# Groups 5 and 7 of an SSD layer projected ahead of the scans in half products, and three parts of the output projection beside the last three scans

## The chip, the cores and the metric

The kernel runs on one core of a Trainium2 chip. The metric is the device time of one execution, in microseconds (us); the median of several runs stands for a kernel. Engines are named as in the profile: TensorE (PE, with its weight load PEld), VectorE (DVE), ScalarE (ACT), GpSimd (POOL), and SyncE (SP), which here does nothing but issue DMA transfers, in order.

## What is computed

One inference step of a trunk of two layers with a final RMS norm: 1024 prompt tokens and 8 x 8 sample tokens, 1088 in all, of width 1024, in fp32. Layer 0 is a Mamba-2 (SSD) layer, layer 1 a pooling layer. The change concerns layer 0, which in the reference is:

```
zxbcdt = h @ w_in                                   # h: modulated RMS norm of x
conv = conv_b + sum(xp[:, k:k + L] * conv_w[k] for k in range(4))
xbc_act = silu(conv)                                # x (2048), B and C (8 groups x 128 each)
dt = softplus(dt_raw + dt_bias); A = -exp(a_log)
y, new_ssm = ssd_scan(xs, dt, A, Bm, Cm, ssm_prev)  # h_t = exp(dt A) h + dt x B^T, y = h C
y = y + d_skip * xs
gated = (y * silu(z)).reshape(b, L, 8, 256)
gated = gated * rsqrt(mean(gated * gated, axis=-1) + EPS) * norm_g
out = gated @ w_out
x = x + (1 + gate) * out
```

The scan runs in eight groups (4 heads, one B and one C of 128 states each), the prompt in 8 chunks of 128 tokens, the samples in one step from a given state. Each group has its own RMS norm over its 256 channels.

## The kernel before

**Products.** Channels lie on the 128 partitions, tokens along the columns. Every matrix product is three fp32r matmuls on a high and a low half of each operand: hi x hi, hi x lo, lo x hi (`mm3`, `mm1`, lines 178, 179 and 180). A projection tile of 128 outputs is made in three chunks of columns `CH` (364, 364, 360), 8 k-tiles each: 72 matmuls. A second form takes two tiles at once, split into a 2 x 2 block product with seven half products in place of eight (`fast_pair`, `product`, lines 945 to 947): each half product has 4 k-tiles, two column quarters of 272 and three matmuls, so a pair takes 7 x 24 = 168 narrower matmuls in place of 144. It needs sums of the activations (slots `T`, built once) and sums of the weights, split three products ahead on VectorE and GpSimd (line 172).

**Front.** `FRONT` names eight pairs made in half products ahead of the scans: the gates z of groups 2 to 7, and group 0 whole (`b` is the pair B and C, `x` the pair of x tiles). z of groups 0 and 1 are made plain. A gate goes through `z_chunk` (tanh on ScalarE, one product on VectorE, which gives 2 silu) and is stored to DRAM. A B, C or x tile goes through `conv_tile`: one tap on ScalarE, three on VectorE over 1112 columns (line 343), tanh, one product on VectorE (line 347).

**Scans.** `scan_group(g)` is a generator of steps: per chunk transposes of B and x, decays from a broadcast of the log sums (`acb`, its DMA at line 497), states and rows on TensorE; at the end the samples, the gate product, the group's norm (the sum of squares by matmul at line 677, Ln and Exp on ScalarE, whose result `rsd` is stored), and the rows, unscaled, stored to DRAM (`gyd`). `ssd_layer` weaves scan g, for g of 0 to 6, with the twelve units (a unit is one chunk of a tile, 24 matmuls) of the projection of group g + 1. Scan 7 is woven with output part 0, whose 24 units have 12 matmuls each.

**Output projection.** `w_out` has 16 k-tiles, two for each group; `PARTS` cuts them in four parts of four. For each k-tile `op_stage` loads the row and the broadcast of its group's rs, `op_split` multiplies (line 702) and makes the halves `gh` (line 706) and `gl` (line 707), with norm_g as a scale. `op_unit` makes the 12 matmuls of a chunk and adds the product, times the gate, to x (line 726, for sample columns 729 and 731). x stays in eight slots. Parts 1 and 2 (`op_paced`) and 3 (`last_part`, which also sums the squares for the next norm) follow scan 7 in `ssd_out`. The slots (`NSLOT_A` of 30) hold all of these tiles; the halves `hh`, `hl` of h take 16 of them until the last projection is done. Small blocks of the adaLN projection (`ada_do`) stand between units.

**Order.** The scheduler gives each engine its instructions in the order in which the code emits them, moved where priorities allow; SP carries nearly every load and store of this layer in one queue, in order.

Of the kernel before, what the change touches and what calls it, by code (L numbers as in the profile page):

```python
# [14 lines left out]
P = 128  # L15
# [10 lines left out]
XA = 4  # L26
# [3 lines left out]
AE = 1  # L30
# [16 lines left out]
FRONT = (("z", 2), ("z", 3), ("z", 4), ("z", 5), ("b", 0), ("z", 6), ("x", 0), ("z", 7))  # L47
# [46 lines left out]
class Build:  # L94
# [95 lines left out]
    def setup(self):  # L190
# [24 lines left out]
        self.eps = cp.tile([P, 2], F32, tag="eps", name="eps")  # L215
        nc.vector.memset(self.eps[:, 0:1], EPS)
        nc.vector.memset(self.eps[:, 1:2], 4.0 * EPS)
# [3 lines left out]
        self.psh = cp.tile([P, 16], F32, tag="psh", name="psh")  # L221
        nc.vector.tensor_scalar(self.psh, self.vec[:, V_PS:V_PS + 16], 0.5, None, op0=ALU.mult)
# [16 lines left out]
    def ada_block(self, src):  # L239
# [16 lines left out]
        mp = self.cp.tile([P, 256], F32, tag="mp", bufs=2, name=self.name("mp"))  # L256
# [31 lines left out]
    def ms_log(self, ss, rst, a, n, inv, eps, tag="tr", bufs=2, more=None):  # L288
# [6 lines left out]
        self.nc.scalar.activation(rst[:, a:a + n], ps[:, :n], AF.Ln, bias=self.eps[:, eps:eps + 1], scale=inv)  # L295
# [39 lines left out]
    def conv_tile(self, ti, raw, dst, ncv):  # L335

        nc, n = self.nc, 1112
        rv = raw[:, 1027:1115].rearrange("p (b w) -> p b w", w=11)
        w = [self.cwh[:, 4 * ti + k:4 * ti + k + 1] for k in range(4)]
# [4 lines left out]
        nc.gpsimd.tensor_copy(ncv[:, 0:1, :], raw[:, 1024:1027].unsqueeze(1))  # L344
        nc.gpsimd.tensor_copy(ncv[:, 1:9, :], rv[:, :, 8:11])
# [5 lines left out]
    def raw_tile(self):  # L351
        return self.gp.tile([P, 1115], F32, tag="raw", bufs=3, name=self.name("raw"))
# [13 lines left out]

    def proj_end(self, G, ii, raw):
        dst = self.slots.get("xbc")
        self.conv_tile(G["ti"][ii], raw, dst, G["ncv"][:, ii])
        G["out"].append(dst)  # L370
        if ii == 3:
            self.nc.sync.dma_start(self.io["ncT"][G["g"]], G["ncv"])

    def proj_group(self, G):

        nc = self.nc
        for ii in range(4):
            w = self.stream_next()
            raw = self.proj_begin(G, ii)
            ada = self.ada_do(self.ada_plan[G["g"], ii]) if (G["g"], ii) in self.ada_plan else iter(())  # L380
            for c, (a, n) in enumerate(CH):
                ps = self.mm_tile()
                self.mm3(ps, w, self.hn, CH[c])
                pn = min(a + n, NP) - a
                nc.scalar.activation(raw[:, 3 + a:3 + a + pn], ps[:, :pn], AF.Identity)
                if pn < n:
# [1102 lines left out]
    def op_paced(self, l, acts, nxt):  # L1489
# [6 lines left out]
        for _ in nxt:  # L1496
            pass
# [284 lines left out]
```

## Time and profile before

| | |
|---|---|
| runs | 1655.09, 1656.16, 1655.75 us; median 1655.75 |
| the profiled execution | 1654.85 us, span 1653.1 us |
| granted TensorE clock, mean | 0.992 |
| TensorE busy | 1614.4 us, 98% of the span |
| VectorE, ScalarE, GpSimd busy | 1313.0, 831.6, 469.1 us (79%, 50%, 28%) |
| moved by DMA | 251.07 MB, 152 GB/s on average |

The span is the time from the first to the last record of the profile; the 1.75 us that the execution's time has more lie around it. The 40 slices of the page are 41 us each. TensorE's digit is 9 in all of them but the first, the twentieth (from 785 us, where scan 7 begins) and the last. The front lasts to about 270 us, the scans 0 to 7 to about 860, output parts 1 to 3 follow, then the pooling layer.

### The profile page before, as it was taken

To read this page: it belongs to the slowest core of one execution; us is meant where nothing else is said; L and a number is where in the kernel's file an instruction comes from. 1 tells how busy PE (TensorE), PEld (TensorE's weight loads), DVE (VectorE), ACT (ScalarE), POOL (GpSimd) and SP (SyncE) were. 2 spreads that over 40 slices of the span, in tenths; PEclk is the share of its full clock that TensorE was granted. 3 is DMA by queue.
4 is the path that set the end of the run, shared out by engine and by line. 5 is a ranking of instruction groups with operands and counts; after the bars stand their busy time and mean duration, and the time that the engine had idled before them with its cause. 6 is when DMAs were issued, how large, how long until landed. Compare 5 with 4: busy or idle time off the path is not lost.

```text
span 1653.1 us, 30634 instructions
## 1 busy us (share of the span) xinstructions
PE 1614.4 (98%) x11965; PEld 1537.2 (93%) x11965; DVE 1313.0 (79%) x2176; ACT 831.6 (50%) x1618; POOL 469.1 (28%) x503
## 2 busy tenths in 40 slices
PE   8999999999999999999899999999999999999997
PEld 6899999989898989998789999999999999999997
DVE  6897587878787787888787656999999968577886
ACT  6544335777677767777442116633333234233364
POOL 0124441313131222313010012366666640000241
PEclk9999999999999999999899999999999999999999
DMA  8423226454453534354867123033323359655773
GB/s 342 160 79 111 91 68 219 128 166 145 158 171 120 182 105 146 125 158 141 290 227 254 42 80 133 28 114 124 111 87 112 126 184 364 201 148 173 171 171 120
DMA packets 115969, 251.07 MB, mean 152 GB/s; under 512 B 17488, under 2 KB 58608, under 8 KB 115824
## 3 DMA queue, kind: packets, MB, share of 16 engines
q1 hardware_dynamic: 111792, 236.39, 42.1%
q0 software_dynamic: 4032, 12.72, 4.4%
q8 instruction: 94, 1.54, 0.4%
q14 instruction: 51, 0.42, 0.1%
HBM read 188.87 MB, written 57.98 MB: 149 GB/s over the span
## 4 chain that ended last, share of the span: by engine, by line
PE 64%; DVE 11%; POOL 8%; issue 8%; DMA 5%; ACT 3%; SPq 0%; DVEq 0%; ACTq 0%; POOLq 0%
PE mm L178 12%; PE mm L179 12%; PE mm L180 11%; PE st L947 3%; PE st L945 3%; PE st L946 3%; PE op L1162 2%; PE op L1163 2%; PE op L1161 2%; POOL w L172 2%; PE y L578 2%; PE S L557 2%; PE y L582 1%; PE am L252 1%; POOL sw L911 1%
## 5 line engine op out<-in xcount | busy, mean ns | idle before, releaser
L178 PE MATMUL mm<-hh,wh 128*128 128x364 f32 x720 | 243.0, 337 | 0.0
L180 PE MATMUL mm<-hh,wl 128*128 128x364 f32 x720 | 237.6, 330 | 0.0
L179 PE MATMUL mm<-hl,wh 128*128 128x364 f32 x720 | 237.0, 329 | 0.0
L947 PE MATMUL st<-hh,w 128*128 128x272 f32 x704 | 203.2, 289 | 0.8 <-DVE w L172 0.8
L946 PE MATMUL st<-hl,w 128*128 128x272 f32 x704 | 203.1, 289 | 0.0
L945 PE MATMUL st<-hh,w 128*128 128x272 f32 x704 | 202.9, 288 | 0.0
L947 PE MATMUL st<-t,w 128*128 128x272 f32 x528 | 152.4, 289 | 3.7 <-POOL w L172 2.9
L946 PE MATMUL st<-t,w 128*128 128x272 f32 x528 | 152.2, 288 | 0.7 <-DVE t L1352 0.7
L945 PE MATMUL st<-t,w 128*128 128x272 f32 x528 | 151.7, 287 | 0.0
L178 PEld LDWEIGHTS mm<-hh,wh 128*128 128x128 f32 x720 | 135.3, 188 | 11.1 <-issue 8.1
L343 DVE SCALAR_TENSOR_TENSOR raw<-raw,cwh,raw 128x1112 f32<-128x1112 f32 x96 | 134.1, 1397 | 6.9 <-ACT raw L341 6.4
L179 PEld LDWEIGHTS mm<-hl,wh 128*128 128x128 f32 x720 | 135.5, 188 | 2.0 <-issue 1.6
L180 PEld LDWEIGHTS mm<-hh,wl 128*128 128x128 f32 x720 | 135.3, 188 | 1.4 <-issue 1.4
L565 POOL TENSOR_TENSOR hd<-h,cd 128x256 f32<-128x256 f32 x56 | 51.7, 924 | 290.8 <-DVE h L566 149.2
L947 PEld LDWEIGHTS st<-hh,w 128*128 128x128 f32 x704 | 132.4, 188 | 1.0 <-DVE w L172 1.0
L945 PEld LDWEIGHTS st<-hh,w 128*128 128x128 f32 x704 | 132.8, 189 | 0.3 <-issue 0.3
L946 PEld LDWEIGHTS st<-hl,w 128*128 128x128 f32 x704 | 132.5, 188 | 0.0
L178 PE MATMUL mm<-gh,wh 128*128 128x364 f32 (+1 forms) x384 | 128.3, 336 | 4.0 <-ACT gh L706 4.0
L1162 PE MATMUL op<-b,w 128*128 128x272 f32 x448 | 128.9, 288 | 1.0 <-DVE b L1091 1.0
L1161 PE MATMUL op<-b,w 128*128 128x272 f32 x448 | 129.5, 289 | 0.0
L179 PE MATMUL mm<-gl,wh 128*128 128x364 f32 (+1 forms) x384 | 127.5, 332 | 1.7 <-DVE gl L707 1.7
L1163 PE MATMUL op<-b,w 128*128 128x272 f32 x448 | 129.0, 288 | 0.0
(294 smaller groups left out, 4581.6 us busy)
## 6 DMA issues: line engine op xcount, KB each, us to landing
wr<-win SPq DMA_DIRECT2D x48, 512.0 KB, 3.6
acb<-acd SPq DMA_DIRECT2D x64, 256.0 KB, 3.6
wr<-pin SPq DMA_DIRECT2D x32, 512.0 KB, 3.9
wr<-pout SPq DMA_DIRECT2D x28, 512.0 KB, 5.3
wr<-pout POOLq DMA_DIRECT2D x20, 512.0 KB, 5.8
x<-xT SPq DMA_DIRECT2D x16, 544.0 KB, 6.7
zsd<-z SPq DMA_DIRECT2D x16, 544.0 KB, 3.1
z<-zsd SPq DMA_DIRECT2D x16, 544.0 KB, 4.0
```

The costliest lines, as they stand in the source:

```text
L172: eng.tensor_tensor(out=lo, in0=src, in1=hi.bitcast(F32), op=ALU.subtract)
L178: nc.tensor.matmul(ps[:, :n], hi[:, k, :], ah[:, a:a + n], start=first, stop=False)
L179: nc.tensor.matmul(ps[:, :n], hi[:, k, :], al[:, a:a + n], start=False, stop=False)
L180: nc.tensor.matmul(ps[:, :n], lo[:, k, :], ah[:, a:a + n], start=False, stop=last)
L343: nc.vector.scalar_tensor_tensor(out=acc[:, :n], in0=raw[:, k:k + n], scalar=w[k], in1=acc[:, :n], op0=ALU.mult, op1=ALU.add)
L565: nc.gpsimd.tensor_tensor(out=hd, in0=h[-1], in1=cd.unsqueeze(2).to_broadcast([P, 4, 64]), op=ALU.mult)
L945: nc.tensor.matmul(ps[c][:, :QUART], hi[:, k], xh[:, t], start=(k == 0), stop=False)
L946: nc.tensor.matmul(ps[c][:, :QUART], hi[:, k], xl[:, t], start=False, stop=False)
L947: nc.tensor.matmul(ps[c][:, :QUART], lo[:, k], xh[:, t], start=False, stop=(k == 3))
L1161: nc.tensor.matmul(ps[:, :QUART], hi[:, k], xh, start=k == 0, stop=False)
L1162: nc.tensor.matmul(ps[:, :QUART], hi[:, k], xl, start=False, stop=False)
L1163: nc.tensor.matmul(ps[:, :QUART], lo[:, k], xh, start=False, stop=k == 7)
```

## The change

The list `FRONT` gets four more pairs: B, C and x of groups 5 and 7 are now projected in half products too. Their conv results are stored to DRAM (`xbd`) and loaded back at step 8 of the scan before. The groups projected beside scans are those of `BESIDE` (1, 2, 3, 4, 6). A table `FILL` says how many units stand behind each step of each scan. Behind the projections stand parts 0, 1 and 2 of the output projection: 24, 24 and 16 units beside scans 5, 6 and 7, and the rest of part 2 behind scan 7, the last six of its units after the norm of group 7. Only part 3 stands behind it whole.

For that, the product with rs and norm_g moves into the end of each scan (line 720 of the changed kernel), one step later than the norm; the rows are stored scaled, and `op_split` is a copy and a subtraction. The last group's rows stay in their slots (`last_rows`). x no longer has eight slots: each tile is loaded (two tiles ahead, `XA`), added to, and stored to `x1d` by parts 0 and 1, and loaded again by the next. The last tile projected beside scans goes k by k over three PSUM tiles, so that a pair of slots of h comes free at each k, and the rows of part 0 are loaded and split there (`self.prep`).

In tiles made ahead of the scans, and in all gates, silu is one ScalarE instruction; the taps of such a conv tile run over 1024 columns and 64 sample columns. A gate is applied over halves (544 columns) in place of quarters or chunks. With silu in place of twice silu the eps of the group norm is EPS and no longer 4 EPS, and a halved copy of a scale in the pooling layer is gone. There are four `raw` buffers in place of three and one `mp` buffer in place of two; the adaLN blocks stand beside tiles of projections 1 to 4 and 6, and two in part 0. The conv tiles made beside scans keep tanh.

```diff
-XA = 4
+PREP = ((6, 10, 14, 18, 21), (9, 12, 15, 18, 21))
...
-FRONT = (("z", 2), ("z", 3), ("z", 4), ("z", 5), ("b", 0), ("z", 6), ("x", 0), ("z", 7))
+FRONT = (("z", 2), ("z", 3), ("z", 4), ("b", 5), ("x", 5), ("z", 5), ("b", 7), ("x", 7), ("z", 6), ("b", 0), ("x", 0),
+         ("z", 7))
+BESIDE = (1, 2, 3, 4, 6)
+
+FILL = (((1,) * 10 + (2,),) * 4 + ((1,) * 9 + (4, 5),) + ((3, 2, 2, 2, 2, 2, 2, 2, 2, 2, 3),) * 2 + ((2, 2, 2, 1, 1, 1, 1, 1, 2, 2, 1),))
 WIDE = 1223
...
+        if not scan:
+            w = [self.vec[:, V_CW + 4 * ti + k:V_CW + 4 * ti + k + 1] for k in range(4)]
+            sd = dst[:, NP:TOK].rearrange("p (b i) -> p b i", i=8)
+            for k in range(4):
+                for d, r in ((dst[:, :NP], raw[:, k:k + NP]), (sd, rv[:, :, k:k + 8])):
+                    if k:
+                        nc.vector.scalar_tensor_tensor(out=d, in0=r, scalar=w[k], in1=d, op0=ALU.mult, op1=ALU.add)
+                    else:
+                        nc.scalar.activation(d, r, AF.Identity, bias=self.vec[:, V_CB + ti:V_CB + ti + 1], scale=w[0])
+            nc.scalar.activation(dst, dst, AF.Silu)
...
+            if (G["g"], ii) == (BESIDE[-1], 3):
+
+                ps = [self.mm_tile() for _ in CH]
+                for k in range(8):
+                    for c in range(3):
+                        self.mm1(ps[c], w, k, self.hn[k], CH[c], k == 0, k == 7)
+                    self.slots.free(*self.hn[k])
+                    if k:
+                        next(self.prep, None)
+                    if k < 7:
+                        yield
+                for c in range(3):
+                    self.proj_evict(G, ii, raw, ps[c], c)
+                yield
+                return
...
         nc.sync.dma_start(self.rsd[g], rs.rearrange("(j q) n -> j q n", q=32)[:, 0, :])
+        self.slots.free(*sq)
+        rst = self.slots.get("rs")
+        nc.sync.dma_start(rst, self.rsd[g].rearrange("j n -> (j n)").unsqueeze(0).to_broadcast([P, TOK]))
+        yield
+
         for q in range(2):
-            nc.sync.dma_start(self.gyd[2 * g + q], xs[q])
-        self.slots.free(*sq, *xs)
+            nc.vector.scalar_tensor_tensor(out=xs[q], in0=xs[q], scalar=self.vec[:, V_SG + 2 * g + q:V_SG + 2 * g + q + 1], in1=rst,
+                                           op0=ALU.mult, op1=ALU.mult)
+            if g < 7:
+                nc.sync.dma_start(self.gyd[2 * g + q], xs[q])
+        self.slots.free(rst)
+        if g < 7:
+            self.slots.free(*xs)
+        else:
+            self.last_rows = xs
         yield
...
+    def op_stage(self, k):
+
+        if k > 13:
+            return self.last_rows[k - 14]
+        raw = self.slots.get("gr", short=True)
+        self.nc.sync.dma_start(raw, self.gyd[k])
+        return raw
+
+    def op_split(self, raw):
+        hi, lo = self.slots.get("gh", F32R, short=True), self.slots.get("gl", F32R, short=True)
+        self.nc.scalar.activation(hi, raw, AF.Copy)
+        self.nc.vector.tensor_tensor(out=lo, in0=raw, in1=hi.bitcast(F32), op=ALU.subtract)
         self.slots.free(raw)
         return hi, lo
...
+    def op_part_load(self, part, out):
+
+        st = None
+        for k in range(*PARTS[part]):
+            nx = self.op_stage(k)
+            if st is not None:
+                out.append(self.op_split(st))
             st = nx
             yield
+        out.append(self.op_split(st))
+        yield
...
+        return self.nc.scalar.activation(dst[:, a:a + n], src, AF.Silu)
...
+                        if g:
+                            t = G["out"].pop()
+                            nc.sync.dma_start(self.xbd[g][ii + i], t)
+                            sl.free(t)
...
+        T, rest = {0: self.G[0]["out"]}, iter(())
+        self.x = [None] * 8
+        self.acts = [[] for _ in PARTS]
+        self.prep = self.op_part_load(0, self.acts[0])
+        self.fill = self.beside(T)
+        for g in range(8):
+            sc = self.scan_group(g, T[g])
+            for i, n in enumerate(FILL[g]):
+                next(sc)
+                for j in range(n):
+                    next(self.fill)
+                    if i in (0, 3) and j == 0:
+                        next(rest, None)
+                if i == 8 and g + 1 in self.G:
+                    T[g + 1] = [sl.get("xbc") for _ in range(4)]
+                    for t, d in zip(T[g + 1], self.xbd[g + 1]):
+                        nc.sync.dma_start(t, d)
+            rest = sc
+        self.prep = self.op_part_load(3, self.acts[3])
+        self.out_unit()
+        next(rest)
+        for _ in range(2):
+            next(self.fill)
+        self.out_unit()
         for _ in rest:
             pass
...
+    def out_unit(self):
+
+        ins = next(self.fill, None)
+        with self.tc.issue_after(ins.ins) if ins else contextlib.nullcontext():
+            next(self.prep, None)
+        return ins
+
+    def beside(self, T):
+
+
+        for g in BESIDE:
+            G = self.proj_open(g)
+            T[g] = G["out"]
+            yield from self.proj_group(G)
+        for p in range(3):
+            for _ in self.prep:
+                pass
+            self.prep = iter(())
+            if p < 2:
+                self.prep = self.op_part_load(p + 1, self.acts[p + 1])
+            for i, ins in enumerate(self.op_units(p)):
+                if p < 2 and i in PREP[p]:
+                    with self.tc.issue_after(ins.ins) if ins else contextlib.nullcontext():
+                        next(self.prep, None)
+                yield ins
+            self.free_acts(self.acts[p])
 
     def free_acts(self, acts):
         for hi, lo in acts:
...
+    def load_x(self, p, d):
+        if d < 8:
+            self.x[d] = self.slots.get("x")
+            self.nc.sync.dma_start(self.x[d], (self.x1d if p else self.io["xT"])[d])
+
+    def op_units(self, p):
+
+        for d in range(XA):
+            self.load_x(p, d)
         for d in range(8):
-            if ada and d + XA < 8:
-                self.load_x(d + XA)
-            if len(acts) > 4:
-                w = self.stream_next()
-            elif d % 2 == 0:
+            if d > 7:
+                if (p, d) in self.ada_late:
+                    for _ in self.ada_do(self.ada_late[p, d]):
+                        pass
+                    yield None
+                continue
+            self.load_x(p, d + XA)
+            if d % 2 == 0:
                 ws = self.stream_pair()
-            blk = self.ada_do(ada[d - 1]) if 0 < d <= len(ada) else iter(())
+            blk = self.ada_do(self.ada_late[p, d]) if (p, d) in self.ada_late else iter(())
             for i, ch in enumerate(CH):
-                ins = self.op_unit(l, self.x, d, w if len(acts) > 4 else ws[d % 2], acts, ch)
+                ins = self.op_unit(0, self.x, d, ws[d % 2], self.acts[p], ch)
                 if i:
                     next(blk, None)
                 yield ins
+            if p < 2:
+                self.nc.sync.dma_start(self.x1d[d], self.x[d])
+                self.slots.free(self.x[d])
```

The first place is on TensorE, where part 0 begins. Before, that is the start of scan 7, behind the last projection (`mm` of `hh` and `hl`) and one adaLN block (`am`); `tr` are the scan's transposes, `gh` and `gl` the halves of the rows, `wh` and `wl` those of the weights:

```order
L178 MATMUL mm_9116<-hh_734,wh_8782 128x360
L179 MATMUL mm_9116<-hl_735,wh_8782 128x360
L180 MATMUL mm_9116<-hh_734,wl_8783 128x360
L252 MATMUL am_9155<-wr_8786,scp 32x256 x4
L252 MATMUL am_9155<-wr_9001,scp 32x256 x4
L514 MATMUL tr_9214<-xbc_8715,xbc_8510 128x128
L518 MATMUL tr_9214<-kc,xbc_8972 128x128
L178 MATMUL mm_9243<-gh_9171,wh_9005 128x364
L179 MATMUL mm_9243<-gl_9172,wh_9005 128x364
```

In the changed kernel it is the start of scan 5, behind the projection of group 6:

```order
L182 MATMUL mm_8402<-hh_739,wh_8149 128x360
L183 MATMUL mm_8402<-hl_740,wh_8149 128x360
L184 MATMUL mm_8402<-hh_739,wl_8150 128x360
L182 MATMUL mm_8547<-gh_8434,wh_8391 128x364
L183 MATMUL mm_8547<-gl_8435,wh_8391 128x364
L184 MATMUL mm_8547<-gh_8434,wl_8392 128x364
L182 MATMUL mm_8547<-gh_8449,wh_8391 128x364
L183 MATMUL mm_8547<-gl_8450,wh_8391 128x364
L184 MATMUL mm_8547<-gh_8449,wl_8392 128x364
L182 MATMUL mm_8547<-gh_8484,wh_8391 128x364
L545 MATMUL tr_8567<-xbc_8364,xbc_8363 128x128
L549 MATMUL tr_8567<-kc,xbc_8365 128x128
```

Part 0 now follows the last projection directly: seven matmuls of its first unit stand ahead of the scan's first transposes, where before the transposes stood first.

The second place is VectorE at the last rows for part 3. Before, these are multiplied and split during part 2; `x` with `mm` is a unit's addition, `wl` the low half of a weight:

```order
L729 TENSOR_TENSOR gs_10808<-mm_10794,gat_266 128x64
L731 TENSOR_TENSOR x_9199<-x_9199,gs_10808 128x64
L702 TENSOR_TENSOR gr_10759<-gr_10759,rs_10699 128x1088
L136 TENSOR_TENSOR wl_10817<-wr_10712,wh_10816 128x1024
L726 SCALAR_TENSOR_TENSOR x_9200<-mm_10822,gat_266,x_9200 128x364
L707 SCALAR_TENSOR_TENSOR gl_10813<-gr_10759,vec,gh_10812 128x1088
L726 SCALAR_TENSOR_TENSOR x_9200<-mm_10836,gat_266,x_9200 128x364
```

In the changed kernel these rows are group 7's own (`xbc`), scaled at the end of scan 7:

```order
L743 TENSOR_TENSOR gl_11149<-gr_11121,gh_11148 128x1088
L720 SCALAR_TENSOR_TENSOR xbc_10195<-xbc_10195,vec,rs_11068 128x1088
L720 SCALAR_TENSOR_TENSOR xbc_10196<-xbc_10196,vec,rs_11068 128x1088
L764 SCALAR_TENSOR_TENSOR x_10975<-mm_11152,gat_271,x_10975 128x364
L743 TENSOR_TENSOR gl_11167<-xbc_10195,gh_11166 128x1088
L764 SCALAR_TENSOR_TENSOR x_10975<-mm_11170,gat_271,x_10975 128x296
L767 TENSOR_TENSOR gs_11184<-mm_11170,gat_271 128x64
L140 TENSOR_TENSOR wl_11194<-wr_11074,wh_11193 128x1024
L769 TENSOR_TENSOR x_10975<-x_10975,gs_11184 128x64
L743 TENSOR_TENSOR gl_11188<-xbc_10196,gh_11187 128x1088
L764 SCALAR_TENSOR_TENSOR x_10307<-mm_11199,gat_271,x_10307 128x364
```

The two products with rs now stand in front of the additions of part 2's last units (the one from `mm_11152` first), and the two splits, with those additions and a weight's split, behind them.

The third place is SP's queue. Before, in scan 7, beside part 0:

```order
L1487 DMA x_9203<-xT 128x1088
L119 DMA wr_9450<-adaA 128x1024
L497 DMA acb_9481<-acd 128x4x128
L497 DMA acb_9572<-acd 128x4x128
L486 DMA h_157_9767<-h0T 128x1024
L119 DMA wr_9452<-adaA 128x1024
L119 DMA wr_9454<-adaG 128x1024
L486 DMA h_158_9769<-h0T 128x1024
L481 DMA z_9828<-zsd_143 128x1088
```

In the changed kernel, in scan 6, beside part 1:

```order
L1521 DMA x_9667<-x1d_165 128x1088
L528 DMA acb_9703<-acd 128x4x128
L1521 DMA x_9544<-x1d_164 128x1088
L666 DMA hsT<-h_164_9162 128x1024
L713 DMA rsd_126<-z_9208 4x272
L1544 DMA x1d_161<-x_9434 128x1088
L1521 DMA x_9750<-x1d_166 128x1088
L716 DMA rs_9524<-rsd_126 128x1088
L1544 DMA x1d_162<-x_9436 128x1088
L737 DMA gr_9766<-gyd_81 128x1088
L528 DMA acb_9779<-acd 128x4x128
L1521 DMA x_9881<-x1d_167 128x1088
```

Between the loads of `acb` now stand loads and stores of x (lines 1521 and 1544), the store and broadcast of rs (713, 716) and loads of rows (737), where weights of adaLN blocks, states and gates stood.

212 lines of the change are left out of this document (59 added, 153 removed).

## The prediction

> **What bounds the kernel now.** I read the page first, then the busy time by windows, then TensorE's waits in the stretches where its share drops.
>
> ```profile
> span 1653.1 us, 30634 instructions
> PE 1614.4 (98%) x11965; PEld 1537.2 (93%) x11965; DVE 1313.0 (79%) x2176; ACT 831.6 (50%) x1618; POOL 469.1 (28%) x503
> ```
> TensorE (PE) is busy for all but 38.7 us. So the time moves by two things: how long its matmuls take, and how long it stands idle. The windows give both; the columns are the window, its length, busy us and instructions of each engine, granted clock, DMA share and GB/s.
>
> ```profile
> 356.00:430.00 74.00, 73.36 (x567) 66.69 (x566) 58.87 (x91) 53.21 (x118) 18.44 (x27) 1.00 0.49 151
> ...
> 782.00:802.00 20.00, 12.71 (x70) 10.76 (x69) 15.79 (x18) 8.92 (x11) 1.17 (x2) 0.74 0.94 327
> 802.00:882.00 80.00, 78.79 (x631) 67.98 (x630) 63.40 (x124) 34.47 (x76) 10.64 (x10) 1.00 0.72 244
> ...
> 900.00:1000.00 100.00, 100.00 (x605) 100.00 (x604) 58.66 (x106) 22.20 (x25) 11.91 (x15) 1.00 0.21 71
> 1040.00:1050.00 10.00, 7.99 (x38) 7.42 (x38) 8.32 (x29) 8.23 (x25) 4.59 (x13) 0.83 0.00 0
> 1100.00:1200.00 100.00, 100.00 (x801) 99.92 (x800) 94.80 (x144) 30.20 (x60) 65.25 (x51) 1.00 0.34 117
> 178.00:262.00 84.00, 82.62 (x659) 82.40 (x658) 64.05 (x108) 33.49 (x57) 36.20 (x37) 1.00 0.24 83
> ```
> 900:1000 holds plain matmuls alone (128x364 and 128x360): 100 us / 605 = 0.1653 us each. 1100:1200 holds half products alone (128x272): 100 / 801 = 0.1248 us each. 356:430 is one scan with twelve projection units beside it: 73.4 of 74 us busy. 782:802 is the worst stretch inside the kernel, where scan 7 and output part 0 begin: 7.3 us idle, clock 0.74, DMA share 0.94.
>
> ```profile
> PE mm L178 <- ACT gh L706: 4.0, 1, 4.0
> PE tr L518 <- DVE xbc L347: 1.8, 1, 1.8
> PE mm L179 <- DVE gl L707: 1.7, 2, 1.4
> ```
> There (waits between 770 and 882) TensorE waits for the first halves of the scan's rows and for its last conv tile.
>
> **The change: matmuls.** Eight projection tiles leave the plain form: 8 x 72 = 576 matmuls x 0.1653 = 95.2 us. Four pairs come in the half-product form: 4 x 168 = 672 x 0.1248 = 83.9 us. The sum is 11.3 us less. All other matmuls keep their number: the scans now carry 24 + 24 + 24 output units of 12 in place of three projections and part 0.
>
> **Idle that goes.** In 782:802 the rows must pass the norm of the group before (rs), then a product with it, then hi and lo, and slots come free only after the whole last projection. Now the scaling is done inside each scan, part 0 needs only groups 0 and 1, finished long before, and the last projection tile goes k by k, so that slots come free while it runs. The 7.3 us go. The clock of 0.74 over 20 us is 10.4 us at half speed (0.26 x 20 / 0.5); some 3.5 us of those lie in the idle time, so 6.9 us at half speed cost 3.4 us more. Together 10.7 us. What is late next, in the order shown above: the four splits and the last two conv tiles share VectorE.
>
> ```profile
> L343 DVE SCALAR_TENSOR_TENSOR raw<-raw,cwh,raw 128x1112 f32<-128x1112 f32 x96 | 134.1, 1397 | 6.9 <-ACT raw L341 6.4
> L347 DVE SCALAR_TENSOR_TENSOR xbc<-raw,raw 128x1024 f32<-128x1024 f32 x32 | 39.9, 1248 | 13.8 <-ACT raw L346 13.8
> L726 DVE SCALAR_TENSOR_TENSOR x<-mm,gat,x 128x364 f32<-128x364 f32 x64 | 37.9, 593 | 30.1 <-PE mm L180 30.1
> L707 DVE SCALAR_TENSOR_TENSOR gl<-gr,vec,gh 128x1088 fp32r<-128x1088 f32 x16 | 23.2, 1451 | 6.8 <-ACT gh L706 4.9 <-DMA hsT<-h 1.9
> L1044 DVE TENSOR_TENSOR pw<-gin,ph 128x1088 fp32r<-128x1088 f32 x16 | 20.2, 1284 | 0.0
> ```
> Four splits at 1.28 (the kind of L1044), one conv tile at 3 x 1.40 + 1.25 and about 5 us of scan work make 15.6 us; the tile's 72 matmuls and the first units' 24 give 96 x 0.165 = 15.8 us of cover. I take +1.5 us, with ends of 0 and the 7.3 that is there now.
>
> **The tail of scan 7.** Before, parts 1 to 3 stood behind it, and its own rows were wanted only by part 3. Now only six units of part 2 stand between its norm and part 3, which wants them at once.
>
> ```profile
> 779.36 1.28 ACT L300 ACT_TABLE_LOAD   x1 [0.45 <-PE ms L677]
> 780.66 0.49 ACT L680 ACTIVATE z<-ms,eps 128x272 f32<-128x272 f32 x1
> 781.18 0.43 ACT L308 ACTIVATE z<-z 128x272 f32<-128x272 f32 x1
> ```
> ```profile
> spl<-spool SPq DMA_DIRECT2D x16, 60.0 KB, 2.1
> rs<-rsd SPq DMA_DIRECT2D x8, 544.0 KB, 6.1
> ```
> From the norm's matmul: 2.2 us on ScalarE, a small store (spl's 2.1 us is the nearest row), the broadcast at 6.1: 10.4 us. Then VectorE, in the order shown: two products (1.45 each), an eviction (0.59), a split (1.28), about 2.2 us of eviction and weight split, the last split (1.28): 8.3 us, so 18.7. Cover: 6 x 12 + 24 matmuls x 0.165 = 15.9 us. The stall is 2.8 us, with ends of 0 (broadcast in 3.3) and 7 (in 10). The unit queued behind the two products on VectorE waits too: a PSUM tile comes free only with it.
>
> ```profile
> 1042.97 0.44 PE L178 MATMUL pl<-hh,wh 128*128 128x360 f32 x1 [1.99 <-ACT hh L318]
> ```
> A gap of this size has a price beside it: after 1.99 us idle the clock in 1040:1050 is 0.83, which is 3.4 us at half speed, 1.7 us. I add it: 4.5 us for the tail. The Trainium skill, "TensorE: Matmul & The Clock Gate", HAM oscillation, asks only that no gap exceed about 3.4 us; by that rule the stall would cost no clock, and the forecast would be 1.7 us lower. The row above speaks against it. The Trainium skill, "ScalarE: Activation LUTs", What ACT_TABLE_LOAD costs, adds 1.38 us of drain to each load; that would put the tail at 5.9 us. Here the next ScalarE instruction starts 1.30 us after the load, so the trace does not agree.
>
> **The front.** Four of twelve pairs are new. The window 178:262 is b, z, x, z of group 0: VectorE 64.1 of 84 us. A conv tile costs it 3 x 1.40 + 1.25 + 0.2 = 5.65 us now and 3 x 1.46 = 4.4 with silu (three products over 1024 and 64 columns). In that window two conv pairs take 22.6 us of it and two gates 9.2 (16 products at 0.574), which leaves 8.1 us per pair for the rest; so a conv pair will take 16.9 of 21 us and a gate pair 8.1. VectorE stays below TensorE, but a conv comes as a lump of 8.8 us, and weights are split three products (9 us) ahead.
>
> ```profile
> PE st L947 <- POOL w L172: 1.4, 1, 1.4
> PE st L947 <- DVE w L172: 0.8, 1, 0.8
> ```
> These are all the waits for weights in the front (93 to 270). Four more conv pairs stand here; I take one such wait for all of them, 1.5, with ends of 0 and 6 (one for each). The silu edits elsewhere I put at nothing: ScalarE takes 0.65 us for 544 columns where it took 2 x 0.43, VectorE loses a product, and TensorE at 100% in 1100:1200 covers both. Extra table loads in the front (1.28 us each) lie on a ScalarE that is busy 33 of 84 us.
>
> **Scans 5, 6 and 7.** VectorE in a scan: 58.9 now, less four conv tiles (22.6), plus 24 evictions (16 x 0.59 + 8 x 0.96), four splits (5.1), two scalings (2.9): 61.3 of 74 us. Scan 7 carries only 16 units: TensorE 74 - 49 + 32 = 57 us against about 53 on VectorE, with less slack. The queue is the larger risk.
>
> ```profile
> acb<-acd SPq DMA_DIRECT2D x64, 256.0 KB, 3.6
> x<-xT SPq DMA_DIRECT2D x16, 544.0 KB, 6.7
> gr<-gyd SPq DMA_DIRECT2D x16, 544.0 KB, 5.9
> x<-x1d SPq DMA_DIRECT2D x8, 544.0 KB, 7.5
> wr<-wout SPq DMA_DIRECT2D x16, 512.0 KB, 4.9
> ```
> In scan 6 SyncE's queue holds 30 transfers of 544 KB (x in and out, the rows, the spilled tiles), 8.5 of acb and 10 of 512 KB: 24 MB, where 356:430 moved 151 x 74 = 11 MB. At 327 GB/s, reached in 782:802, that takes 73 us of 74. x is asked for two rows of units (six units, 12 us and the scan's work) ahead, acb one chunk ahead. I take +3 us for the three scans, ends 0 and 15.
>
> **The sum.** The profiled execution took 1654.85 us (span 1653.1 and 1.75 around it), 0.9 below the median of 1655.75. 1654.85 - 11.3 - 10.7 + 1.5 + 4.5 + 1.5 + 3 = 1643.4; beside the median 1644. The ends of the unknown terms give 1633 (all at 0) to about 1662 (all at their worst, which will not meet).
>
> **The rivals.**
> *The wait only moves* (0.17): scan 5 begins with part 0, where the same loads, conv tiles and splits meet. 96 x 0.165 of cover against 15.6 us of VectorE is level, and a row that lands 6 us late tips it. Then 7.3 + 3.4 stay in place of 1.5: 1653.
> *All hidden* (0.13): the broadcast lands in 3.3 us, scans and front as covered as 356:430: 1634.
> *The queue bounds scans 5 and 6* (0.12, the slower side): transfers stand in order on one queue, stores waiting for evictions ahead of loads. In 802:882 it moved 244 GB/s at share 0.72 with TensorE hardly idle, so more was not asked for; 327 at 0.94 is a burst of 20 us with waits. If a scan's 24 MB come at 244 GB/s, each takes 98 us, 24 more: 1644 + 48 = 1692. It decides for slower from 6 us per scan, 24 MB in 80 us: 300 GB/s.
> That nothing moved is excluded by the order of instructions: 672 more half-product matmuls stand on TensorE.
>
> **Chances.** The forecast has 0.58. Up to 0.2% (3.3 us, about what this measurement can tell) counts as same. Faster: 0.58 + 0.13 + 0.10 of the first rival = 0.81; same: 0.07 of it and 0.01 of the queue's = 0.08; slower 0.11. The range 1633 to 1655 holds all but the queue's case and a little above: 8 in 10 or somewhat more.
>
> **What would show it.** Right: 1456 matmuls on each line of the half product; about 0.125 us each; no wait over 2 us where part 0 begins; a wait of 2 to 4 us for the last rows of scan 7 and a dip of the clock behind it; DMA share near 0.9 in scans 5 and 6 with TensorE above 97%. Wrong: TensorE below 95% in those scans with waits that go back to x or acb (the queue), or the clock low where part 0 begins (the wait moved), or waits of more than 2 us for weights in the front.

## The result and the profile after

| | before | changed |
|---|---|---|
| median | 1655.95 us (4 runs) | 1633.49 us (4 runs, 1629.32 to 1633.99) |
| ratio, 95% interval | | 0.9861, 0.9845 to 0.9876 |
| once more, beside the experiments | 1655.07 us | 1631.56 us; 0.9853, 0.9836 to 0.9869 |
| profiled execution | 1654.85 us | 1633.98 us |

The change gains 22.5 us of medians, or 20.9 from profile to profile. The forecast was 11.5 from profile to profile. The page of the changed kernel, its span and its engines, and below them two of the groups:

```profile
span 1632.2 us, 30956 instructions
PE 1601.1 (98%) x12061; PEld 1524.7 (93%) x12061; DVE 1290.3 (79%) x2140; ACT 816.7 (50%) x1565; POOL 495.2 (30%) x527
...
L982 PE MATMUL st<-hh,w 128*128 128x272 f32 x832 | 240.8, 289 | 2.3 <-DVE w L176 2.3
L982 PE MATMUL st<-t,w 128*128 128x272 f32 x624 | 179.6, 288 | 0.0
```
The half-product form stands there as forecast: 832 + 624 = 1456 on each of its lines. TensorE is idle for 31.1 us, 7.6 less than before.

Busy time by windows, changed kernel: the front's half products, scans 5, 6 and 7 (norm to norm), and the half products of the pooling layer.

```profile
96.00:354.60 258.60, 256.26 (x2036) 254.22 (x2035) 195.74 (x329) 110.62 (x176) 124.87 (x119) 1.00 0.30 103
...
739.00:812.80 73.80, 73.80 (x568) 66.69 (x566) 64.82 (x122) 42.57 (x96) 12.16 (x11) 1.00 0.87 297
812.80:882.10 69.30, 69.27 (x528) 65.33 (x526) 59.39 (x114) 36.55 (x84) 13.05 (x11) 1.00 0.93 327
882.10:941.80 59.70, 55.19 (x427) 50.06 (x425) 46.54 (x91) 29.76 (x75) 10.26 (x9) 0.97 0.61 209
...
1057.00:1352.00 295.00, 295.00 (x2352) 295.00 (x2351) 249.29 (x369) 96.51 (x166) 175.80 (x136) 1.00 0.40 133
```
Scans 5 and 6 are full for TensorE at a DMA share of 0.87 and 0.93. Scan 7 is not. TensorE's waits from the first scan to the end of the output projection (changed kernel):

```profile
PE S L588 <- ACT Bt L566: 4.5, 3, 2.3
PE mm L182 <- ACT raw L419: 2.1, 1, 2.1
PE y L613 <- DVE h L593: 1.4, 1, 1.4
```
The second is the beginning of part 0, the first is scan 7. No wait is listed for the tail behind scan 7. The one at `y`, in scan 0, has its like before, where the scan waited 1.4 us for `M`.

Where the time went, by stages cut at the same instructions in both traces (the last ends with TensorE's last matmul, 8.6 and 8.4 us before the span's end):

| stage | before | changed | difference | forecast |
|---|---|---|---|---|
| start, to the first half product | 93.6 | 96.2 | +2.7 | 0 |
| front, to the first chunk of scan 0 | 175.3 | 258.7 | +83.4 | +85.4 |
| scans and output projection | 753.0 | 649.1 | -103.9 | -96.9 |
| pooling layer, plain pair | 54.6 | 53.7 | -0.9 | 0 |
| pooling layer, half products | 297.7 | 294.9 | -2.8 | 0 |
| the rest | 270.4 | 271.2 | +0.8 | 0 |

### The profile page after: what moved, and what is told of

It reads as the page before. It is cut to its first block, busy times and chain, and to the rows that moved or that the text cites. A ratio compares the mean times of both kernels' runs of the same rounds, so it can differ in the third digit from the quotient of the medians.

```text
span 1632.2 us, 30956 instructions
## 1 busy us (share of the span) xinstructions
PE 1601.1 (98%) x12061; PEld 1524.7 (93%) x12061; DVE 1290.3 (79%) x2140; ACT 816.7 (50%) x1565; POOL 495.2 (30%) x527
## 4 chain that ended last, share of the span: by engine, by line
PE 82%; DVE 7%; DMA 5%; issue 3%; ACT 2%; POOL 1%; SPq 0%; DVEq 0%; ACTq 0%; POOLq 0%
PE st L982 11%; PE st L980 11%; PE st L981 11%; PE mm L182 10%; PE mm L184 10%; PE mm L183 10%; DMA acb<-acd 2%; PE op L1197 2%; PE op L1198 2%; PE op L1196 2%; PE y L609 2%; PE S L588 2%; PE y L613 2%; PE am L253 1%; PE tr L549 1%
## 5 line engine op out<-in xcount | busy, mean ns | idle before, releaser
L982 PE MATMUL st<-hh,w 128*128 128x272 f32 x832 | 240.8, 289 | 2.3 <-DVE w L176 2.3
L980 PE MATMUL st<-hh,w 128*128 128x272 f32 x832 | 240.2, 289 | 0.0
L981 PE MATMUL st<-hl,w 128*128 128x272 f32 x832 | 239.7, 288 | 0.0
L982 PE MATMUL st<-t,w 128*128 128x272 f32 x624 | 179.6, 288 | 0.0
L980 PE MATMUL st<-t,w 128*128 128x272 f32 x624 | 179.6, 288 | 0.0
L981 PE MATMUL st<-t,w 128*128 128x272 f32 x624 | 179.2, 287 | 0.0
L182 PE MATMUL mm<-hh,wh 128*128 128x364 f32 (+1 forms) x528 | 178.4, 338 | 0.1
L184 PE MATMUL mm<-hh,wl 128*128 128x364 f32 (+1 forms) x528 | 174.6, 331 | 0.0
L183 PE MATMUL mm<-hl,wh 128*128 128x364 f32 (+1 forms) x528 | 173.7, 329 | 0.0
L174 ACT ACTIVATE w<-wr 128x512 fp32r<-128x512 f32 x104 | 65.6, 631 | 190.4 <-PE st L982 156.8
L982 PEld LDWEIGHTS st<-hh,w 128*128 128x128 f32 x832 | 156.4, 188 | 3.4 <-DVE w L176 3.4
L980 PEld LDWEIGHTS st<-hh,w 128*128 128x128 f32 x832 | 156.7, 188 | 0.3 <-issue 0.3
L184 PE MATMUL mm<-gh,wl 128*128 128x364 f32 (+1 forms) x384 | 127.1, 331 | 0.0
L980 PEld LDWEIGHTS st<-t,w 128*128 128x128 f32 x624 | 117.7, 189 | 0.0
L982 PEld LDWEIGHTS st<-t,w 128*128 128x128 f32 x624 | 117.3, 188 | 0.0
```

The lines of the kernel that those rows point to most:

```text
L174: self.nc.scalar.activation(hi, src, AF.Copy)
L182: nc.tensor.matmul(ps[:, :n], hi[:, k, :], ah[:, a:a + n], start=first, stop=False)
L183: nc.tensor.matmul(ps[:, :n], hi[:, k, :], al[:, a:a + n], start=False, stop=False)
L184: nc.tensor.matmul(ps[:, :n], lo[:, k, :], ah[:, a:a + n], start=False, stop=last)
L980: nc.tensor.matmul(ps[c][:, :QUART], hi[:, k], xh[:, t], start=(k == 0), stop=False)
L981: nc.tensor.matmul(ps[c][:, :QUART], hi[:, k], xl[:, t], start=False, stop=False)
```

## The experiments

Each was timed in five rounds beside the kernel before; the ratios are to that (median 1655.3 us beside the first four, 1655.07 beside the last four).

| kernel | median us | ratio | 95% interval |
|---|---|---|---|
| silu_only | 1650.85 | 0.9969 | 0.9959 to 0.998 |
| norm_order | 1652.57 | 0.9982 | 0.9974 to 0.9991 |
| front8 | 1640.82 | 0.9911 | 0.9897 to 0.9924 |
| evict_first | 1629.21 | 0.984 | 0.9826 to 0.9853 |
| tail_short | 1633.45 | 0.9862 | 0.9844 to 0.988 |
| cd_late | 1624.93 | 0.9818 | 0.9802 to 0.9834 |
| after_again | 1631.56 | 0.9853 | 0.9836 to 0.9869 |
| x_twice | 1651.59 | 0.998 | 0.9968 to 0.9992 |

### The silu edits alone (silu_only)

```diff
     def z_chunk(self, dst, src, a, n):
 
-        nc = self.nc
-        t = self.mt.tile([P, 416], F32, tag="mt", bufs=2, name=self.name("zt"))
-        nc.scalar.activation(t[:, :n], src, AF.Tanh, scale=0.5)
-        return nc.vector.scalar_tensor_tensor(out=dst[:, a:a + n], in0=t[:, :n], scalar=1.0, in1=src, op0=ALU.add, op1=ALU.mult)
+        return self.nc.scalar.activation(dst[:, a:a + n], src, AF.Silu)
```
The conv tiles ahead of the scans, eps and the pooling scale change with it, as in the change.

> The kernel before with the silu edits alone: gates and the conv tiles ahead of the scans by one silu on ScalarE, gates over halves, the factors of two and eps to match; FRONT, the scans and the output parts stay as they were. Theory A (VectorE relieved of a product in each gate and each of these conv tiles splits the weights in time): the waits for weights go, 0.8 and 1.4 us in the front and three of 0.7 to 0.9 in the pooling layer, 4.5 us in all: about 1651.5. Rival (the prediction's: silu is worth nothing where TensorE is the bound): 1656 within 1, with these waits in place.

Measured: 1650.85, 4.5 below the 1655.3 beside it. TensorE's waits in the pooling layer's half products, in the kernel before:

```profile
PE st L947 <- POOL w L172: 1.5, 2, 0.9
PE st L947 <- POOL u L784: 0.8, 1, 0.8
```
In silu_only no wait is left in that stretch. The same two stages by windows, the front's and the pooling layer's half products, in the kernel before:

```profile
93.30:268.50 175.20, 172.11 (x1364) 170.23 (x1363) 141.14 (x251) 69.67 (x132) 71.48 (x65) 1.00 0.29 100
1076.00:1374.00 298.00, 295.64 (x2355) 294.78 (x2354) 270.10 (x425) 99.48 (x193) 176.25 (x136) 1.00 0.39 132
```
and in silu_only:

```profile
96.20:267.90 171.70, 171.29 (x1364) 170.12 (x1363) 109.56 (x197) 69.87 (x116) 71.95 (x65) 1.00 0.29 102
1076.80:1371.00 294.20, 294.20 (x2353) 294.20 (x2352) 247.75 (x369) 96.29 (x165) 176.09 (x136) 1.00 0.39 134
```
The third busy column is VectorE: 141.1 becomes 109.6 us in the front and 270.1 becomes 247.8 in the pooling layer. With VectorE at 91% of a stretch (270.1 of 298.0) the products that prepare weights and windows came late now and then, although TensorE was the bound. The waits in the pooling layer name GpSimd, which is busy 176 us there in both kernels; but GpSimd itself waits for VectorE's splits of weights, 87.8 us in that stretch before and 72.0 in silu_only. That VectorE's relief reaches TensorE on this way is argued from these rows; no run isolates it.

Cut at the same instructions, the front and the pooling stretch are 3.5 us shorter each; the start is 2.9 longer (below). Theory A holds; the prediction's zero does not. The waits for weights in the front are one in silu_only and, with twelve pairs there, five short ones in the changed kernel (line by line):

```profile
PE st L955 <- DVE w L172: 0.4, 1, 0.4
PE st L982 <- DVE w L176: 2.3, 5, 0.6
```

### The table loads at a scan's start (norm_order)

```diff
-        with self.ln_set(mm):
-            nc.scalar.activation(rs, ps[:, :272], AF.Ln, bias=self.eps[:, 1:2], scale=1.0 / 256)
-            self.rstd(rs)
+        nc.scalar.activation(rs, ps[:, :272], AF.Ln, bias=self.eps[:, 1:2], scale=1.0 / 256)
+        self.rstd(rs)
```

> The kernel before without the table load issued by hand ahead of each group's norm, so that Ln stands ahead of the tanh of the first conv tile on ScalarE, as in the changed kernel: 22 table loads in place of 33, two in place of four at the start of each scan. Theory B (the loads delay Bt, and TensorE waits 0.64 us for it in scans 1 to 6): those six waits go, 3.9 us: about 1652. Rival (the transposes or VectorE's xd end as late): 1656 within 1.

ScalarE at the start of scan 2 in the kernel before (the timeline: start, length, line, operation, the idle time before it):

```profile
423.27 1.28 ACT L300 ACT_TABLE_LOAD   x1 [1.40 <-PE ms L677]
424.56 1.28 ACT L346 ACT_TABLE_LOAD   x1
425.85 1.13 ACT L346 ACTIVATE raw<-raw 128x1112 f32<-128x1112 f32 x1
427.00 1.28 ACT L680 ACT_TABLE_LOAD   x1
...
429.17 1.28 ACT L308 ACT_TABLE_LOAD   x1
...
430.80 0.26 ACT L535 ACTIVATE Bt<-tr 128x128 f32<-128x128 f32 x1
```
and at the same place in the changed kernel:

```profile
511.33 1.28 ACT L301 ACT_TABLE_LOAD   x1 [1.07 <-PE ms L708]
512.62 0.49 ACT L711 ACTIVATE z<-ms,eps 128x272 f32<-128x272 f32 x1
513.13 1.28 ACT L359 ACT_TABLE_LOAD   x1
514.42 1.13 ACT L359 ACTIVATE raw<-raw 128x1112 f32<-128x1112 f32 x1
515.46 0.41 ACT L309 ACTIVATE z<-z 128x272 f32<-128x272 f32 x1
```
Before, a load put there by hand for Ln and Exp (L300) was followed at once by the conv tile's tanh, which loaded its own table; Ln and Exp then loaded again. Four loads, 5.1 us, stood ahead of `Bt`, and TensorE waited for it 0.64 us in each of six scans. In the changed kernel Ln comes first, and two loads do: after tanh, Exp needs none. The Trainium skill, "ScalarE: Activation LUTs", Table sets: the hidden batching unit, lists exp with tanh in one set and exp with ln in another; by that, Ln, tanh, Exp need two loads, and the trace of the changed kernel agrees; in the kernel before, Exp (L308) loads again even behind Ln's own load (L680), which a set with both would have spared. In norm_order the kernel before has the changed kernel's order, and its waits from scan 0 to the end of scan 6 are

```profile
PE y L578 <- DVE M L529: 0.7, 1, 0.7
PE S L557 <- ACT Bt L535: 0.2, 1, 0.2
```
The six waits are gone. A scan of 74.27 us takes 73.85: 0.42 less, where the wait was 0.64. Six times that is 2.5, and the median is 2.7 us lower (1.5 to 4.3 by the interval) where 3.9 was expected. Theory B holds, with a gain nearer 3.

### Eight pairs in front, all else changed (front8)

```diff
-FRONT = (("z", 2), ("z", 3), ("z", 4), ("b", 5), ("x", 5), ("z", 5), ("b", 7), ("x", 7), ("z", 6), ("b", 0), ("x", 0),
-         ("z", 7))
-BESIDE = (1, 2, 3, 4, 6)
+FRONT = (("z", 2), ("z", 3), ("z", 4), ("z", 5), ("b", 0), ("z", 6), ("x", 0), ("z", 7))
+BESIDE = (1, 2, 3, 4, 5, 6, 7)
...
```
`FILL` and the units behind scan 7 are changed to match.

> The changed kernel with the eight pairs of before ahead of the scans and groups 5 and 7 projected beside scans as plain matmuls (576 of them in place of 672 half-product ones); part 0 then begins in scan 6, part 1 stands behind scan 7. All else as changed. Theory C (the form of the matmuls is worth its 11 to 12 us, and scan 7 with 24 units in place of 16 has no waits of its own, worth up to 6): 1633.5 + 11.9 = 1645, less up to 6: 1639 to 1645. Rival (what was gained is waits, and the half-product form gains little): within 3 of the changed kernel's 1633.5.

Measured: 1640.82, 7.3 to 9.3 above the two medians of the changed kernel. The front is 87.2 us shorter (171.5 for 258.7), the scans and the output projection 93.8 longer. So the four pairs do pay, by some 8 us; and nearly two thirds of the whole gain (14.5 us) is there without them. Scan 7, with 24 units in place of 16, still waits:

```profile
792.70:869.70 77.00, 73.27 (x525) 66.58 (x523) 64.57 (x118) 33.03 (x71) 10.12 (x9) 0.96 0.77 269
```
That is one wait of 3.7 us on `Bt` and a stretch of 6.8 us at half speed behind it. More units alone do not cover scan 7.

### Where part 0 begins (evict_first)

```diff
-                for k in range(8):
+                for k in range(5):
                     for c in range(3):
                         self.mm1(ps[c], w, k, self.hn[k], CH[c], k == 0, k == 7)
...
                 for c in range(3):
+                    for k in range(5, 8):
+                        self.mm1(ps[c], w, k, self.hn[k], CH[c], False, k == 7)
                     self.proj_evict(G, ii, raw, ps[c], c)
...
```

> The changed kernel with the last tile's last three k-tiles done chunk by chunk, so that its first PSUM tile is read out while the other two are still summed. Theory D (the first unit of part 0 waits 2.06 us for a PSUM tile because its reading stands on ScalarE behind the split of the fourth row, and the clock's dip follows the wait): 2 to 3.7 us less than the changed kernel, 1630 to 1631.5, with no wait over 0.5 us there. Rival (the fourth row's transfer is what is late): the wait moves to its high or low half and the time stays at 1633.5.

ScalarE in the changed kernel, where the last projection ends at 729.9 us:

```profile
729.80 1.11 ACT L742 ACTIVATE gh<-gr 128x1088 fp32r<-128x1088 f32 x1 [0.88 <-DMA gr<-gyd]
730.81 0.68 ACT L556 ACTIVATE M<-acb,tka 128x128 f32<-128x128 f32 x2
731.40 0.19 ACT L574 ACTIVATE cd<-acb 128x4 f32<-128x4 f32 x1
731.50 0.45 ACT L419 ACTIVATE raw<-mm 128x364 f32<-128x364 f32 x1
```
The first PSUM tile is read out (L419) only behind the fourth row's high half, which waited for its transfer. In evict_first the reading stands ahead of it:

```profile
728.28 0.45 ACT L424 ACTIVATE raw<-mm 128x364 f32<-128x364 f32 x1
728.64 1.12 ACT L747 ACTIVATE gh<-gr 128x1088 fp32r<-128x1088 f32 x1
```
The wait for the tile is gone. Another of 1.4 us stands there now, for a low half on VectorE (`gl`): the rival's wait, in a smaller size. The time fell by 2.4 to 4.3 us, and the profile has no half-speed stretch there or in scan 7. Not all of that is this edit's place: from profile to profile 6.1 us went, 0.6 of waiting and 1.7 of clock where part 0 begins, and 2.0 and 1.7 in scan 7, which the edit does not touch. Whether scan 7 gained by it or by chance, the run does not tell.

### Scan 7 (cd_late)

```diff
-            nc.scalar.activation(M[:L, :, :L], M[:L, :, :L], AF.Exp, scale=-1.0)
+            mx = nc.scalar.activation(M[:L, :, :L], M[:L, :, :L], AF.Exp, scale=-1.0)
...
-                nc.scalar.activation(cd, acb[:, :, 127], AF.Exp)
+                with self.tc.issue_after(mx.ins) if g == 7 else contextlib.nullcontext():
+                    nc.scalar.activation(cd, acb[:, :, 127], AF.Exp)
```
It is laid on evict_first.

> The kernel of evict_first with one edge more: in scan 7, cd of a chunk stands on ScalarE behind the Exp of that chunk's M, no longer ahead of it. Theory F (in scan 7 cd, which needs the acb of a chunk further on, stands on ScalarE in front of work on the chunk at hand, so that a late acb stops TensorE for 4.5 us in all): these waits fall to under 1.5 us: 1 to 3 us below evict_first. Rival (acb itself is late for M and ea, wherever cd stands): the waits stay and so does the time, within 1 of evict_first.

ScalarE in scan 7 of the changed kernel, ahead of the longest wait:

```profile
899.98 0.68 ACT L556 ACTIVATE M<-acb,tka 128x128 f32<-128x128 f32 x2
902.23 0.21 ACT L574 ACTIVATE cd<-acb 128x4 f32<-128x4 f32 x1 [1.56 <-DMA acb<-acd]
902.34 0.61 ACT L557 ACTIVATE M<-M 128x512 f32<-128x512 f32 x1
902.88 0.28 ACT L566 ACTIVATE Bt<-tr 128x128 f32<-128x128 f32 x1
```
`cd` takes 0.2 us but needs the acb of a later chunk, and M and `Bt` of the chunk at hand stand behind it. Two of the three waits in scan 7, 2.35 and 1.35 us, end so; the third, 0.8, stands behind `ea`, which itself waited for its acb. With `cd` moved back, all waits of cd_late from scan 0 to the end of the output projection are

```profile
PE mm L183 <- DVE gl L749: 0.7, 1, 0.7
PE y L619 <- DVE h L599: 0.6, 1, 0.6
PE y L619 <- DVE h L603: 0.4, 1, 0.4
PE S L594 <- ACT Bt L571: 0.2, 1, 0.2
```
Scan 7 takes 53.6 us, where it takes 55.9 in evict_first, with waits of 1.85 and 0.7, and 59.7 in the changed kernel. So theory F holds, and in these profiles the edit is worth 2.3 us in scan 7; the median, 1624.93, is 4.3 below evict_first, more than the 1 to 3 expected, and the rest of that is not explained. It is below both kernels of this study: ratio 0.9818, 0.9802 to 0.9834.

### Three units less behind scan 7 (tail_short)

```diff
-FILL = (((1,) * 10 + (2,),) * 4 + ((1,) * 9 + (4, 5),) + ((3, 2, 2, 2, 2, 2, 2, 2, 2, 2, 3),) * 2 + ((2, 2, 2, 1, 1, 1, 1, 1, 2, 2, 1),))
+FILL = (((1,) * 10 + (2,),) * 4 + ((1,) * 9 + (4, 5),) + ((3, 2, 2, 2, 2, 2, 2, 2, 2, 2, 3),) * 2 + ((2, 2, 2, 2, 2, 1, 1, 1, 2, 2, 2),))
```

> The changed kernel with 19 units of the output projection beside scan 7 in place of 16, so that three and not six units of part 2 stand between group 7's norm and part 3. Theory E (the rows' way from the norm to the last split takes 18.3 us, as the prediction had it at 18.7, and is covered by 108 matmuls of 0.166 us, 17.9, where the prediction counted 96): the cover falls by 36 matmuls, 6.0 us, and a wait of about 6 us appears ahead of part 3, with a dip of the clock; scan 7's own waits fall by at most their 4.5. Time: the changed kernel's plus 2 to 8. Rival (the tail has other cover, or the rows come earlier when asked earlier): no wait over 2 us there, time as the changed kernel or up to 4 below.

Measured: 1633.45, no different from the first median of the changed kernel and 1.9 above the second. In its tail TensorE waits four times, 2.9 us in all; the three longest are

```profile
PE mm L183 <- DMA rs<-rsd: 1.0, 1, 1.0
PE mm L182 <- ACT gh L742: 0.8, 1, 0.8
PE mm L183 <- DVE gl L743: 0.6, 1, 0.6
```
Theory E is half right at most. The cover does shrink and waits appear, but not the 6 us, and no dip of the clock stands there. The two traces show why: from the norm's matmul to the end of the last split the rows took 15.2 us (943.8 to 959.0) in place of 18.0. With three units less in that stretch VectorE had fewer additions to make between the rows' own steps; it is busy there for 12.1 us, where it was 14.7. So the rows came earlier, as the rival has it, and the time falls where the rival puts it. (The cover in the changed kernel is 102 matmuls, not 108, and the rows' way 18.0 us, not 18.3; see below.) What part 3 gave up, scan 7 gained (its idle time fell from 4.5 to 2.2).

### The changed kernel again, and the queue (after_again, x_twice)

> The changed kernel once more, beside the others on the same chip. Expected: 1629 to 1634, and half-speed stretches behind different waits than in the first profile (those of 2 us get one in some executions and none in others), so that executions differ by steps of about 1.7 us.

1631.56 (1628.99 to 1632.53); its profile has half-speed stretches of 3.4 us behind waits of 2.5 us in scan 7 and 2.0 at the pooling layer's start, one at 1595 behind a wait of 0.7, and none where part 0 begins, after a wait of 1.3. So the stretches do stand elsewhere, as expected; four times do not show whether they come in steps of 1.7 us.

```diff
-            self.nc.sync.dma_start(self.x[d], (self.x1d if p else self.io["xT"])[d])
+            for _ in range(2):
+                self.nc.sync.dma_start(self.x[d], (self.x1d if p else self.io["xT"])[d])
```

> The changed kernel with each load of x for parts 0, 1 and 2 issued twice (24 loads of 544 KB more, some 8 in each of scans 5, 6 and 7; the second brings the same values). In the changed kernel the DMA share is 0.87 and 0.93 in scans 5 and 6 (297 and 327 GB/s). Theory G (the transfers are hidden, but scan 6 is at the limit): scan 6 grows by about 4.5 MB at 327 GB/s, 14 us, less the 5 us that its share of 0.93 leaves; scan 5 by half of that: 1640 to 1655. Rival (there is room left beside 327 GB/s): less than 3 us more.

Measured: 1651.59, 20.0 above after_again. Scans 5, 6 and 7 of x_twice by windows:

```profile
737.80:814.70 76.90, 75.95 (x568) 66.54 (x566) 61.69 (x120) 33.76 (x74) 11.60 (x11) 1.00 0.89 313
814.70:888.90 74.20, 72.37 (x526) 64.47 (x524) 58.09 (x111) 39.12 (x92) 10.46 (x11) 1.00 0.95 332
888.90:960.40 71.50, 62.40 (x439) 52.22 (x439) 51.26 (x99) 35.13 (x89) 10.31 (x11) 0.95 0.87 296
```
Theory G holds in the sum, not in its places: scan 5 grows by 3.1, scan 6 by 4.9, and the backlog falls due in scan 7, which grows by 11.8. The transfers of the change are hidden; 24 x 544 KB more, 13 MB, are not. Each addition to such a tile also waits for two loads in place of one (TensorE's longest wait, 5.3 us in scan 7, goes back to one of them), and the run does not separate that from the rate.

## Why the prediction was wrong

The direction and the largest terms were right; the gain came out nearly twice as large. Two steps of the prediction failed by more than 4 us each: the cover of the tail was counted short, so that the stall put at +4.5 did not come, and the silu edits, put at nothing, gained 4.5. Six waits that no term of the sum looked at went too. The median is that of the rival *All hidden* (1634), but by luck: that rival wanted the broadcast in 3.3 us and scans without waits, while the broadcast took 3.9 us (948.4 to 952.3), and part 0's beginning and scan 7 lost 10 us that other gains made up. Two figures of the prediction's working do not add up, without weight for the forecast: all unknown terms at their worst give 1668, not 1662 (the front's 6 is left out), and the 288 matmuls for which it takes off 49 us are 47.6 us at 0.1653.

**Matmuls, -11.3: right.** 1456 on each line of the half product, 0.125 us each. The front grew by 83.4 us, where 83.9 stood for the matmuls alone; front8 gives 7 to 9 us for this part with the waits that go with it.

**The stall at the last projection, -10.7: right.** No wait of 4 us is left. **Its residue, +1.5: place right, engine wrong, size short.** 2.1 us of waiting and 1.7 of clock; the reading of a PSUM tile on ScalarE was late, not the splits on VectorE. evict_first shows both: that wait goes, and VectorE's is the next, 1.4 us. The clock is low where part 0 begins (0.86 from 730 to 742 us), the prediction's own sign for its first rival, but 3.8 us were lost there and not 10.7.

**The tail, +4.5: the cover is the first step that failed.** The rows' way was priced well: from the norm's matmul at 942.1 to the end of the last split at 960.05 it took 18.0 us against 18.7. VectorE's part of it in the changed kernel:

```profile
952.70 2.61 DVE L720 SCALAR_TENSOR_TENSOR xbc<-xbc,vec,rs 128x1088 f32<-128x1088 f32 x2
955.23 0.59 DVE L764 SCALAR_TENSOR_TENSOR x<-mm,gat,x 128x364 f32<-128x364 f32 x1
955.73 1.28 DVE L743 TENSOR_TENSOR gl<-xbc,gh 128x1088 fp32r<-128x1088 f32 x1
...
958.77 1.28 DVE L743 TENSOR_TENSOR gl<-xbc,gh 128x1088 fp32r<-128x1088 f32 x1
```
The cover was counted short. 96 matmuls of 0.165 us, 15.9, stand in the prediction; TensorE had 102 to do before it needed the last split, at 0.168 us, and 0.6 us of the norm's own: 17.7. They are the 72 of part 2 and ten of each of three units of part 3, which were open at once, one in each PSUM tile. TensorE's stops there add up to 0.3 us, in place of 2.8, and the clock did not dip: 0.3 for the 4.5. tail_short shows the same balance from the other side.

**Silu, 0: the second step that failed.** The prediction put the silu edits "at nothing" because TensorE is at 100% in 1100:1200. That window has no waits; the stretch around it (1076 to 1374) had three, 2.3 us, and VectorE at 91%, and the front's, 3.1 us, were relieved too. silu_only measures 4.5 us. **The front, +1.5: new waits right, the balance wrong.** The new waits for weights came, 2.3 us in five, within the ends of 0 and 6. But the 3.1 us of waits that were there before went with VectorE's relief, so that the front's waits fell by 0.8 us in place of growing by 1.5.

**Not in the sum: the six waits for `Bt`, 3.9.** They were in the trace of before, and the changed kernel has 24 table loads where 33 stood. No term of the sum looked at the order of ScalarE's work in the scans, since ScalarE is busy only half of the time. norm_order, with 22 loads, measures 2.7.

**Scans 5 to 7, +3: size short, place wrong.** Scans 5 and 6, where the queue was the danger, lost nothing. The queue's rival is dismissed by 327 GB/s at share 0.93 over the whole of scan 6: the prediction took 244 GB/s of a stretch that asked for no more as what the queue can give. Scan 7, with the fewest transfers of the three, lost 4.5 us and 1.7 of clock. In the trace 3.7 of the 4.5 end behind one short instruction in a queue served in order; moved back, in cd_late, it took the 1.85 us with it that were left of them in evict_first.

**The clock's price, 1.7 us behind a wait of 2 us: right in some executions only.** The wait of 1.95 to 2.04 us at the pooling layer's start is in all ten profiles of this study; six have a stretch at half speed behind it; the first of the changed kernel has none. The Trainium skill, "TensorE: Matmul & The Clock Gate", HAM oscillation, asks for gaps under about 3.4 us; by these profiles a gap of 2 us already costs in six of ten. Another section of that page of the Trainium skill, Part 1: The HAM clock gate, says that the clock's window runs free of the program, so that the same kernel differs from run to run; with that the two profiles of the changed kernel agree, one with such a stretch and one without.

The sum with what was measured, for the scans: -95.2 and -10.7, + 3.8, + 6.2, - 3.9 is -99.8 of the -103.9. TensorE's idle time in this stage fell from 14.3 to 8.2 us, which is 1.5 more than these terms hold, in short waits. The other 2.6 us lie in its busy time and are not settled by a run, nor is the cause of the 2.7 us that the start grew; it grew alike in silu_only (96.4 for 93.6), so it comes with the silu edits, and in both 1.8 of it is one wait (last section).

## What to carry to other kernels

TensorE at 98% does not make relief of other engines worthless: read the list of short waits over the whole stretch, not the busy share of one good window, and price each engine's relief by the waits that name it or an engine that waits for it. Look at the order of each engine's instructions for what stands in front of a late one: two table loads too many, a tile's reading behind a split, or 0.2 us of work that needs a later chunk's data cost some 2 to 4 us each, and moving them took a few lines. When a stall is priced against cover, count as cover all that is ready in the units behind it, not only the units in front, and remember that the cover's own work on other engines lengthens the way that it covers.

## What was not expected of the hardware

In the start of the changed kernel, two of the differences on VectorE (L1375, 128x544) run while GpSimd prepares weights, and one later:

```profile
58.88 3.53 DVE L1375 TENSOR_TENSOR x<-x,x 128x544 f32<-128x544 f32 x2
...
66.47 0.71 DVE L1375 TENSOR_TENSOR x<-x,x 128x544 f32<-128x544 f32 x1
```
The two take 3.53 us, the one 0.71. GpSimd is busy from 56.5 to 61.8 us in that trace. The kernel before has the same beside GpSimd: with it busy from 56.9 to 61.8, `hl` and `x` over 128x1024 take 2.30 and 2.31 us, and 1.28 at other times. TensorE waits 1.8 us for a low half from VectorE, until 65.1, in the changed kernel and in silu_only, but not in the kernel before. The Trainium skill, "GPSIMD Engine Reference", Specifications, says that GpSimd shares VectorE's way to SBUF for instructions with two inputs there; these rows agree, but no run varied it.

DMA moved 327 GB/s at a share of 0.93 for 69 us, and 332 at 0.95 in x_twice for 74 us, on loads and stores mostly of 256 to 544 KB, nearly all issued from one queue.
